# Keeping the turned input: one raw transpose of x, its norm factor applied afterwards, and the turned columns kept in DRAM for the residual

## The chip, the cores and the metric

The kernel runs on one core of one Trainium2 chip. The metric is the device time of one execution in microseconds. The time before is 1986.39 us, the median of three runs (1981.85, 1986.65 and 1986.39). "Faster", "same" and "slower" are told apart at 0.3% of that, about 6 us.

## What is computed

One layer of a hybrid decoder runs on two groups that share all weights: a prompt of 256 tokens and a sample group of 8 sequences with one token each, so 264 columns in all. In short:

```python
h = rmsnorm(x) * norm_mix                      # x: (256, 2048) prompt, (8, 2048) sample
q, k, v, z, xbc, dt, qm, gates = split(h @ w_in)
a_out = sliding_window_attention(q, k, v)      # 16 heads, 4 kv heads, window 128
s_out = ssd(xbc, z, dt)                        # Mamba-2 branch
m_out = cross_attention(qm, memory)            # memory = rmsnorm(mem_prompt) @ w_mem_kv
merged = g0 * (a_out @ w_up_swa) + g1 * (s_out @ w_up_ssd) + g2 * (m_out @ w_up_mem)
x = x + merged @ w_out                         # the residual: x itself is needed again here
x = x + (silu(rmsnorm(x) @ w_gate) * (rmsnorm(x) @ w_up)) @ w_down
```

All data are float32. The kernel keeps nearly float32 precision by splitting each operand of the large products into a rounded high part and a low part, and adding three products: high by high, high by low, low by high.

## The kernel before, in words

Activations are kept *turned*: the 2048 features lie on partitions, as `KT` = 16 blocks of 128, and the 264 tokens (256 prompt, `NP`; 8 sample, `NS`) lie along the free dimension. A large product is a list of *units*. One unit is 512 KB of weights (two blocks of 128 rows by 512 columns): a DMA on SP's queue into `raw` (four buffers), a copy on ScalarE that rounds it into `hi` (line 167, function `split`), a subtraction on VectorE that gives `lo` (line 168), and then 24 matmuls on TensorE (line 146), or 12 wider ones for the memory product. `feed(i)` runs ahead of unit `i`: it issues the loads of up to four units more and splits up to three.

The units stand in this order: 32 for the memory tokens' keys and values (`pmem`), then the products with `w_in` (`pin`) mixed with the three upward products (`pua`, `pum`, `pus`), then 32 for `w_out` (`pout`, four groups `i` of 512 output features), then the feed-forward part (`pg`, `pu`, `pdn`).

Everything that is not a large product is *side work*: generators in two lists, `side` and `slow`. After each unit the main loop gives `side` 1.0 and `slow` 0.75 of credit, and each `yield` of a generator takes some. That fixes the order in which instructions are written down; a scheduler then reorders them by their dependencies, their priority (the written order) and a model of the engines' times, and each engine runs its own resulting list in order. The first three tasks of `side` are `mem_norm`, `prep_x` and `consts`. `mem_norm` must be written before unit 7, `prep_x` before unit 30, `consts` before the first `pin` unit.

`prep_x` makes the split input of all `pin` products, `hh` and `hl` (16 blocks each of 128 by 264). Before the change it loads the rows of x into four tiles of 128 by 1024 and the sample's rows into two tiles of 8 by 1024, squares them on ScalarE with a row sum, gets the factor `r` = 1/sqrt(mean + eps) by a few small VectorE operations (`rsqrt`), multiplies the rows by it in place on VectorE, and then, for each block `k`, turns three pieces on TensorE (two of 128 by 128, one of 8 by 128) into one PSUM tile `xT`. From that ScalarE writes `hh(k)` (scaled by the norm gain) and VectorE writes `hl(k)`.

`load_x(i)`, which is called when group `i` of `w_out` begins, loads 512 columns of x once more, unscaled (`xg` and `xgs`), turns them by twelve transposes into PSUM tiles `xTr`, and copies them on ScalarE into `xT`, the residual that `after_out(i)` adds to the product.

Buffers that matter: `t1` (four tiles of 128 by 264), `t4` and `ev` (four tiles each of 128 by 4 by 264), and the PSUM tag `s` with three banks that all transposes and small matmuls share. `move_rows` copies two caches from DRAM to DRAM; it is written down with the last group of `w_out`.

Of the kernel before, what the change touches and what calls it, by code (L numbers as in the profile page):

```python
# [8 lines left out]
F32 = mybir.dt.float32  # L9
# [3 lines left out]
AF = mybir.ActivationFunctionType  # L13
ALU = mybir.AluOpType
AX = mybir.AxisListType
# [3 lines left out]
P = 128  # L19
D = 2048  # L20
NP = 256
NS = 8
NT = NP + NS
KT = D // P
# [48 lines left out]
def tile_hybrid_decoder_step(  # L73
# [9 lines left out]
    nc = tc.nc  # L83
    act = nc.scalar.activation
    V = nc.vector
# [6 lines left out]
    dr = ctx.enter_context(tc.tile_pool(name="dr", bufs=1, space=DRAM))  # L92
# [4 lines left out]
    def nm(s):  # L97
        uid[0] += 1
        return f"{s}_{uid[0]}"
# [4 lines left out]
    def t4(name, dt=F32):  # L104
        return tp.tile([P, 4 * NT], dt, tag="t4", name=nm(name), bufs=4)

    def ev(name):
        return tp.tile([P, 4, NT], F32, tag="ev", name=nm(name), bufs=4)
# [16 lines left out]
    def t2(name, dt=F32):  # L125
        n = 512 if dt in (F32, F32R) else 1024
        return tp.tile([P, n], dt, tag="t2", name=nm(name), bufs=4)

    def t1(name, dt=F32):
        return tp.tile([P, NT], dt, tag="t1", name=nm(name), bufs=4)  # L130

    def tiny(name, n):
        assert n <= 64
        return tp.tile([P, 64], F32, tag="tiny", name=nm(name), bufs=9)[:, 0:n]

    def const(shape, name, dt=F32, tag=None):
        return cp.tile(shape, dt, tag=tag or name, name=name)
# [4 lines left out]
    def sps(name):  # L142
        return pq.tile([P, 512], F32, tag="s", name=nm(name))

    def mm(out, lhsT, rhs, start=True, stop=True):
        nc.tensor.matmul(out, lhsT=lhsT, rhs=rhs, start=start, stop=stop)  # L146

    def tr(out, in_):
        n = in_.shape[0]
        nc.tensor.transpose(out, in_, ident[0:n, 0:n])  # L150

    def rsqrt(v, n, parts=P, alloc=None):

        alloc = alloc or tiny
        y = alloc("rs_y", n)[0:parts]
        a = alloc("rs_a", n)[0:parts]
        V.tensor_scalar(y.bitcast(I32), v.bitcast(I32), 1, None, op0=ALU.logical_shift_right)
        V.tensor_scalar(y.bitcast(I32), y.bitcast(I32), -1.0, MAGIC, op0=ALU.mult, op1=ALU.add)
        for _ in range(3):
            V.tensor_tensor(a, y, y, op=ALU.mult)  # L160
            V.scalar_tensor_tensor(a, a, -0.5, v, op0=ALU.mult, op1=ALU.mult)
            V.scalar_tensor_tensor(y, a, 1.5, y, op0=ALU.add, op1=ALU.mult)
        return y

    def split(hi, lo, src):

        act(hi, src, AF.Copy)  # L167
        V.tensor_tensor(lo, src, hi.bitcast(F32), op=ALU.subtract)  # L168


    ident = const([P, P], "ident")
    make_identity(nc, ident)
    ones = const([P, P], "ones")
# [19 lines left out]
    xs_rows = x_sample.rearrange("b s d -> (b s) d")  # L193
# [7 lines left out]
    g_mem, g_mix = vgc[:, 0:16], vgc[:, 16:32]  # L201
# [198 lines left out]

    hh, hl = Feat("hh"), Feat("hl")

    def prep_x():
        x_t = {}
        for h in range(2):
            for t in range(2):
                m = (lm if t else ld)("x")
                nc.gpsimd.dma_start(m, x_prompt[0, t * P:(t + 1) * P, h * 1024:(h + 1) * 1024])
                x_t[t, h] = m
                yield 1.3  # L410
        xs = {h: ev("xs").rearrange("p c n -> p (c n)")[0:NS, 0:1024] for h in range(2)}
        for h in range(2):
            nc.gpsimd.dma_start(xs[h], xs_rows[:, h * 1024:(h + 1) * 1024])
            x_t[2, h] = xs[h]
        jk = t2("jkx", BF16)
        ss = tiny("ssx", 6)
        V.memset(ss, 1.0)
        for t in range(3):
            n = P if t < 2 else NS
            for h in range(2):  # L420
                act(jk[0:n], x_t[t, h], AF.Square, accum_out=ss[0:n, 2 * t + h:2 * t + h + 1])
            yield 0.5
        v = tiny("vx", 3)
        V.tensor_tensor(v, ss[:, 0:6:2], ss[:, 1:6:2], op=ALU.add)
        V.tensor_scalar(v, v, 1.0 / D, EPS, op0=ALU.mult, op1=ALU.add)
        r = rsqrt(v, 3)
        yield 1.5
        for t in range(3):
            n = P if t < 2 else NS
            for h in range(2):  # L430
                V.tensor_scalar(x_t[t, h], x_t[t, h], r[0:n, t:t + 1], None, op0=ALU.mult)
            yield 1.2
        for k in range(KT):
            ps = sps("xT")
            h, c = k // 8, (k % 8) * P
            for t in range(3):
                n = P if t < 2 else NS
                tr(ps[:, t * P:t * P + n], x_t[t, h][:, c:c + P])
            act(hh(k), ps[:, 0:NT], AF.Copy, scale=g_mix[:, k:k + 1])
            V.scalar_tensor_tensor(hl(k), ps[:, 0:NT], g_mix[:, k:k + 1], hh(k).bitcast(F32),  # L440
                                   op0=ALU.mult, op1=ALU.subtract)
            yield 0.4


    tri = const([P, P], "tri")
# [989 lines left out]
    x2 = {}  # L1435

    def load_x(i):
        xt = t4("xg")[:, 0:1024].rearrange("p (t c) -> p t c", t=2)
        nc.gpsimd.dma_start(xt, x_prompt[0, :, 512 * i:512 * (i + 1)].rearrange("(t p) c -> p t c", p=P))
        xs = t2("xgs")[0:NS]  # L1440
        nc.gpsimd.dma_start(xs, xs_rows[:, 512 * i:512 * (i + 1)])
        o = t4("xT").rearrange("p (c n) -> p c n", c=4)
        for c in range(4):
            ps = sps("xTr")
            for t in range(2):
                tr(ps[:, t * P:(t + 1) * P], xt[:, t, c * P:(c + 1) * P])
            tr(ps[:, NP:NT], xs[:, c * P:(c + 1) * P])
            act(o[:, c], ps[:, 0:NT], AF.Copy)
        x2[f"r{i}"] = o

    def after_out(i):
# [28 lines left out]
    def before_out(i):  # L1480
        load_x(i)
        if i == 3:
            move_rows()
# [67 lines left out]

    side.add("m", mem_norm())
    side.add("x", prep_x())
    side.add("c", consts())
    side.add("Mp", mem_prompt_work(), ["qm"])
# [61 lines left out]
```

## Time and profile before

| | before |
|---|---|
| median of three runs | 1986.39 us |
| the profiled execution | 1981.87 us |
| its span, first to last instruction | 1980.1 us |
| TensorE matmuls busy | 1937.3 us, 98% of the span |
| VectorE busy | 1159.3 us, 59% |
| ScalarE busy | 970.8 us, 49% |
| GpSimd busy | 122.6 us, 6% |
| mean granted TensorE clock | 0.994 of full speed |
| moved by DMA | 400.78 MB, 202 GB/s |

In the lines of the profile PE is TensorE, PEld its weight loads, DVE VectorE, ACT ScalarE, POOL GpSimd and SP the engine whose queue issues the weight loads. "L146" is line 146 of the kernel. An arrow `out<-in` names the tile written and the tiles read. A window is given in microseconds from the first instruction.

### The profile page before, as it was taken

The page shows a single profiled execution, that of the slowest core. Times are in us where ns is not written, and L with a number is a line of the kernel's source. Part 1 is how long each engine was busy: PE and PEld are TensorE (multiplying, and loading weights), DVE is VectorE, ACT ScalarE, POOL GpSimd, SP SyncE. Part 2 cuts the span into 40 slices and gives each one's busy share as a digit, 9 for nine tenths or more (in the row PEclk, how much of TensorE's full clock was granted, in tenths as well). Part 3 has the DMA queues.
Part 4 walks back from the last instruction along what each step waited for, and adds up shares of the span by engine and source line. Part 5 has one row for each costly group of instructions (what it writes and reads, how often), then busy time and mean ns, then how long its engine had stood idle before and what let it go on. Part 6 is the DMA issues. An engine that isn't in the chain of part 4 may idle for free.

```text
span 1980.1 us, 37652 instructions
## 1 busy us (share of the span) xinstructions
PE 1937.3 (98%) x15436; PEld 1871.3 (95%) x15436; DVE 1159.3 (59%) x2217; ACT 970.8 (49%) x1419; POOL 122.6 (6%) x241
## 2 busy tenths in 40 slices
PE   8999999999898989999999999999999999999999
PEld 6799998889898989899999999999999999999998
DVE  6645577656486858568455556555545555445553
ACT  6544446656665575655444444444334444334443
POOL 3000110010101202111000000000000000000000
PEclk9999999999999999999999999999999999999999
DMA  8576677677678878779666556665556665566653
GB/s 283 192 221 206 204 210 232 199 220 232 172 203 223 249 195 252 243 268 334 186 192 191 183 164 178 181 181 180 181 181 174 184 185 180 182 179 180 181 188 130
DMA packets 190974, 400.78 MB, mean 202 GB/s; under 512 B 13491, under 2 KB 15714, under 8 KB 190664
## 3 DMA queue, kind: packets, MB, share of 16 engines
q1 hardware_dynamic: 169856, 324.13, 53.4%
q0 software_dynamic: 20944, 74.23, 12.6%
q8 instruction: 121, 1.98, 0.4%
q14 instruction: 53, 0.43, 0.1%
HBM read 376.53 MB, written 24.06 MB: 202 GB/s over the span
## 4 chain that ended last, share of the span: by engine, by line
PE 84%; DMA 7%; DVE 3%; issue 3%; ACT 1%; POOL 0%; SPq 0%; ACTq 0%; POOLq 0%
PE pin L146 22%; PE pu L146 13%; PE pdn L146 13%; PE pg L146 13%; PE pout L146 5%; PE pus L146 5%; PE pmem L146 5%; DMA raw<-in_w_in_dram 3%; PE pum L146 2%; DMA ld<-in_state_ssm_dram 1%; DVE lo L168 1%; PE pua L146 1%; DVE ld L1226 1%; DMA acs_d<-acsT 1%; PE po L146 1%
## 5 line engine op out<-in xcount | busy, mean ns | idle before, releaser
L168 DVE TENSOR_TENSOR lo<-raw,hi 128x1024 fp32r<-128x1024 f32 (+1 forms) x626 | 746.7, 1195 | 650.7 <-ACT hi L167 649.7
L167 ACT ACTIVATE hi<-raw 128x1024 fp32r<-128x1024 f32 (+1 forms) x626 | 646.0, 1036 | 869.4 <-PE pin L146 190.3
L146 PE MATMUL pin<-hh,hi 128*128 128x264 f32 x1728 | 494.7, 289 | 15.8 <-ACT hi L167 15.6
L146 PE MATMUL pin<-hl,hi 128*128 128x264 f32 x1728 | 493.3, 288 | 0.0
L146 PE MATMUL pin<-hh,lo 128*128 128x264 f32 x1728 | 483.7, 288 | 5.5 <-DVE lo L168 5.2
L146 PEld LDWEIGHTS pin<-hh,hi 128*128 128x128 f32 x1728 | 328.4, 190 | 22.9 <-ACT hi L167 18.2
L146 PEld LDWEIGHTS pin<-hh,lo 128*128 128x128 f32 x1728 | 322.2, 190 | 10.1 <-DVE lo L168 8.3
L146 PEld LDWEIGHTS pin<-hl,hi 128*128 128x128 f32 x1728 | 328.3, 190 | 3.3 <-issue 2.5
L146 PE MATMUL pdn<-fah,hi 128*128 128x264 f32 x704 | 199.7, 285 | 0.0
L146 PE MATMUL pdn<-fal,hi 128*128 128x264 f32 x704 | 199.4, 285 | 0.0
L146 PE MATMUL pu<-h2h,hi 128*128 128x264 f32 x704 | 199.4, 284 | 0.0
L146 PE MATMUL pu<-h2l,hi 128*128 128x264 f32 x704 | 199.3, 284 | 0.0
L146 PE MATMUL pg<-h2l,hi 128*128 128x264 f32 x704 | 199.1, 285 | 0.0
L146 PE MATMUL pg<-h2h,hi 128*128 128x264 f32 x704 | 198.4, 284 | 0.0
L146 PE MATMUL pdn<-fah,lo 128*128 128x264 f32 x704 | 197.0, 284 | 0.0
L146 PE MATMUL pu<-h2h,lo 128*128 128x264 f32 x704 | 196.6, 284 | 0.0
L146 PE MATMUL pg<-h2h,lo 128*128 128x264 f32 x704 | 196.1, 284 | 0.0
L146 PEld LDWEIGHTS pdn<-fah,hi 128*128 128x128 f32 x704 | 132.7, 189 | 0.1
L146 PEld LDWEIGHTS pu<-h2h,hi 128*128 128x128 f32 x704 | 132.7, 189 | 0.0
L146 PEld LDWEIGHTS pg<-h2h,hi 128*128 128x128 f32 x704 | 132.7, 188 | 0.0
L146 PEld LDWEIGHTS pdn<-fal,hi 128*128 128x128 f32 x704 | 132.6, 188 | 0.1
L146 PEld LDWEIGHTS pu<-h2l,hi 128*128 128x128 f32 x704 | 132.6, 188 | 0.0
(511 smaller groups left out, 2964.7 us busy)
## 6 DMA issues: line engine op xcount, KB each, us to landing
raw<-in_w_in_dram SPq DMA_DIRECT2D x218, 512.0 KB, 4.5
raw<-in_w_gate_dram SPq DMA_DIRECT2D x88, 512.0 KB, 3.7
raw<-in_w_up_dram SPq DMA_DIRECT2D x88, 512.0 KB, 3.9
raw<-in_w_down_dram SPq DMA_DIRECT2D x88, 512.0 KB, 4.0
raw<-in_w_mem_kv_dram SPq DMA_DIRECT2D x32, 512.0 KB, 5.2
raw<-in_w_up_ssd_dram SPq DMA_DIRECT2D x32, 512.0 KB, 3.8
raw<-in_w_out_dram SPq DMA_DIRECT2D x32, 512.0 KB, 3.7
ld<-in_cache_mem_k_dram POOLq DMA_DIRECT2D x16, 512.0 KB, 5.5
```

Source lines behind the costliest of these rows:

```text
L146: nc.tensor.matmul(out, lhsT=lhsT, rhs=rhs, start=start, stop=stop)
L167: act(hi, src, AF.Copy)
L168: V.tensor_tensor(lo, src, hi.bitcast(F32), op=ALU.subtract)
L1226: V.scalar_tensor_tensor(h[:, b], bb[:, b], dx[:, b:b + 1], h[:, b], op0=ALU.mult, op1=ALU.add)
```

## The change

`prep_x` turns x unscaled. The sample's 8 rows are loaded as one tile of 128 by 128 (16 pieces of 128 features for each of 8 rows, so partition 8k+b holds piece k of row b) and turned by one transpose into `xsT`. The sums of squares of the sample rows, which now lie spread over 16 partitions each, are gathered by a matmul of `ones` with a selection matrix `sel`; the prompt's factors are spread along the free dimension by a matmul of `ones` with a diagonal `dgx`. The result is one tile `rb` of 128 by 264 that holds the norm factor of each column. For each block two pieces are turned, ScalarE copies them to a tile `raw` (tag `xr`), VectorE multiplies by gain and `rb` into `xn`, and `split` makes `hh(k)` and `hl(k)`. Every four blocks the raw tile is written to a DRAM tensor `xT_d`. `load_x(i)` is now one load from `xT_d`.

```diff
+    xT_d = dr.tile([P, KT, NT], F32, name="xT_d")
     def prep_x():
         x_t = {}
+        xs = t1("xs")[:, 0:P]
+        nc.gpsimd.dma_start(xs, xs_rows.rearrange("b (k n) -> k b n", n=P))
         for h in range(2):
             for t in range(2):
                 ... (load of x_t[t, h], as before)
                 yield 1.3
-        xs = {h: ev("xs").rearrange("p c n -> p (c n)")[0:NS, 0:1024] for h in range(2)}
-        for h in range(2):
-            nc.gpsimd.dma_start(xs[h], xs_rows[:, h * 1024:(h + 1) * 1024])
-            x_t[2, h] = xs[h]
         jk = t2("jkx", BF16)
         ss = tiny("ssx", 6)
-        V.memset(ss, 1.0)
-        for t in range(3):
-            n = P if t < 2 else NS
+        act(jk[:, 0:P], xs, AF.Square, accum_out=ss[:, 4:5])
+        for t in range(2):
             for h in range(2):
-                act(jk[0:n], x_t[t, h], AF.Square, accum_out=ss[0:n, 2 * t + h:2 * t + h + 1])
+                act(jk, x_t[t, h], AF.Square, accum_out=ss[:, 2 * t + h:2 * t + h + 1])
             yield 0.5
+        sel = tiny("sel", NS)
+        V.tensor_reduce(sel, ident.rearrange("p (k b) -> p b k", b=NS), axis=AX.X, op=ALU.add)
+        V.tensor_scalar(sel, sel, ss[:, 4:5], None, op0=ALU.mult)
+        ps = sps("xn")
+        tr(ps[:, 0:P], xs)
+        mm(ps[:, P:P + NS], ones, sel)
+        v = tiny("vx", 10)
+        ... (prompt sums and the eight gathered sums into v)
+        xsT = t1("xsT")[:, 0:P]
+        act(xsT, ps[:, 0:P], AF.Copy)
         V.tensor_scalar(v, v, 1.0 / D, EPS, op0=ALU.mult, op1=ALU.add)
-        r = rsqrt(v, 3)
+        r = rsqrt(v, 10)
         yield 1.5
-        for t in range(3):
-            n = P if t < 2 else NS
-            for h in range(2):
-                V.tensor_scalar(x_t[t, h], x_t[t, h], r[0:n, t:t + 1], None, op0=ALU.mult)
-            yield 1.2
-        for k in range(KT):
-            ps = sps("xT")
-            h, c = k // 8, (k % 8) * P
-            for t in range(3):
-                n = P if t < 2 else NS
-                tr(ps[:, t * P:t * P + n], x_t[t, h][:, c:c + P])
-            act(hh(k), ps[:, 0:NT], AF.Copy, scale=g_mix[:, k:k + 1])
-            V.scalar_tensor_tensor(hl(k), ps[:, 0:NT], g_mix[:, k:k + 1], hh(k).bitcast(F32),
-                                   op0=ALU.mult, op1=ALU.subtract)
-            yield 0.4
+        dg = t1("dgx")[:, 0:256]
+        for t in range(2):
+            V.tensor_scalar(dg[:, t * P:(t + 1) * P], ident, r[:, t:t + 1], None, op0=ALU.mult)
+        ps = sps("rbx")
+        mm(ps[:, 0:NP], ones, dg)
+        rb = t1("rb")
+        act(rb[:, 0:NP], ps[:, 0:NP], AF.Copy)
+        V.tensor_copy(rb[:, NP:NT], r[:, 2:10])
+        yield 0.5
+        for q in range(4):
+            raw = ev("xr")
+            V.tensor_copy(raw[:, :, NP:NT], xsT[:, 32 * q:32 * q + 32].rearrange("p (c b) -> p c b", b=NS))
+            for c in range(4):
+                k = 4 * q + c
+                h, o = k // 8, (k % 8) * P
+                ps = sps("xT")
+                for t in range(2):
+                    tr(ps[:, t * P:(t + 1) * P], x_t[t, h][:, o:o + P])
+                act(raw[:, c, 0:NP], ps[:, 0:NP], AF.Copy)
+                tm = t1("xn")
+                V.scalar_tensor_tensor(tm, raw[:, c], g_mix[:, k:k + 1], rb, op0=ALU.mult, op1=ALU.mult)
+                split(hh(k), hl(k), tm)
+                yield 0.6
+            nc.gpsimd.dma_start(xT_d[:, 4 * q:4 * q + 4], raw)
...
     def load_x(i):
-        xt = t4("xg")[:, 0:1024].rearrange("p (t c) -> p t c", t=2)
-        nc.gpsimd.dma_start(xt, x_prompt[0, :, 512 * i:512 * (i + 1)].rearrange("(t p) c -> p t c", p=P))
-        xs = t2("xgs")[0:NS]
-        nc.gpsimd.dma_start(xs, xs_rows[:, 512 * i:512 * (i + 1)])
         o = t4("xT").rearrange("p (c n) -> p c n", c=4)
-        for c in range(4):
-            ps = sps("xTr")
-            for t in range(2):
-                tr(ps[:, t * P:(t + 1) * P], xt[:, t, c * P:(c + 1) * P])
-            tr(ps[:, NP:NT], xs[:, c * P:(c + 1) * P])
-            act(o[:, c], ps[:, 0:NT], AF.Copy)
+        nc.gpsimd.dma_start(o, xT_d[:, 4 * i:4 * i + 4])
         x2[f"r{i}"] = o
```

More of the change, by code (lines that the diff above doesn't have):

```diff
@@ L422, in prep_x @@
             yield 0.5
-        v = tiny("vx", 3)
-        V.tensor_tensor(v, ss[:, 0:6:2], ss[:, 1:6:2], op=ALU.add)
+        sel = tiny("sel", NS)
[5 more added lines that the diff above has]
+        v = tiny("vx", 10)
+        V.tensor_tensor(v[:, 0:2], ss[:, 0:4:2], ss[:, 1:4:2], op=ALU.add)
@@ L425, in prep_x @@
+        V.tensor_copy(v[:, 2:10], ps[:, P:P + NS])
+        xsT = t1("xsT")[:, 0:P]
+        act(xsT, ps[:, 0:P], AF.Copy)
         V.tensor_scalar(v, v, 1.0 / D, EPS, op0=ALU.mult, op1=ALU.add)
-        r = rsqrt(v, 3)
+        r = rsqrt(v, 10)
         yield 1.5
-        for t in range(3):
-            n = P if t < 2 else NS
-            for h in range(2):
-                V.tensor_scalar(x_t[t, h], x_t[t, h], r[0:n, t:t + 1], None, op0=ALU.mult)
-            yield 1.2
-        for k in range(KT):
-            ps = sps("xT")
-            h, c = k // 8, (k % 8) * P
-            for t in range(3):
-                n = P if t < 2 else NS
-                tr(ps[:, t * P:t * P + n], x_t[t, h][:, c:c + P])
-            act(hh(k), ps[:, 0:NT], AF.Copy, scale=g_mix[:, k:k + 1])
-            V.scalar_tensor_tensor(hl(k), ps[:, 0:NT], g_mix[:, k:k + 1], hh(k).bitcast(F32),
-                                   op0=ALU.mult, op1=ALU.subtract)
-            yield 0.4
+        dg = t1("dgx")[:, 0:256]
```

## The prediction

> **What bounds the kernel now.** I read the busy shares first, then the two stages that the change touches by windows, then what ends the waits there.
>
> ```profile
> PE 1937.3 (98%) x15436; PEld 1871.3 (95%) x15436; DVE 1159.3 (59%) x2217; ACT 970.8 (49%) x1419; POOL 122.6 (6%) x241
> 63.90:113.80 49.90, 49.90 (x228) 38.80 (x228) 31.37 (x56) 24.65 (x35) 3.89 (x7) 1.00 0.62 204
> 600.00:700.00 100.00, 89.09 (x750) 86.21 (x748) 69.90 (x208) 54.96 (x102) 16.92 (x20) 0.98 0.86 234
> 700.00:800.00 100.00, 93.02 (x777) 91.27 (x778) 67.89 (x176) 62.62 (x103) 12.80 (x16) 0.95 0.81 230
> 1094.00:1198.00 104.00, 104.00 (x828) 100.98 (x827) 57.01 (x82) 49.74 (x78) 1.42 (x2) 1.00 0.54 175
> ```
>
> The window columns are: length, then busy time of TensorE's matmuls, its weight loads, VectorE, ScalarE and GpSimd, the granted clock, the DMA share and GB/s. The first window is the stretch in which `prep_x` multiplies and turns x, the last is the `w_out` stage. In both TensorE has no idle time, VectorE and ScalarE are busy for half to two thirds, DMA for 0.62 and 0.54. TensorE has gaps between 600 and 800, where the change writes nothing. A busy matmul row is modelled, so I ask who waits for whom (engine, line, releaser: total, times, longest):
>
> ```profile
> ACT hi L167 <- PE pmem L146: 20.4, 14, 1.9
> ACT hi L167 <- PE pout L146: 43.2, 23, 1.9
> ```
>
> These are the waits of 60 to 130 us and of the `w_out` stage. The rounding of the next weights waits until matmuls have released a `hi` buffer; so TensorE sets the pace, and not the load or the split. Time taken off TensorE's list in these two stages is time off the kernel, and nothing else in them is, as long as TensorE has its operands.
>
> **The change: TensorE.** The chain of waits runs through TensorE there, so its pieces (start, duration) are what the transposes cost on the path, without the overlap that single rows carry. First the shares by line of 76 to 122 us and of 1050 to 1230 us, then pieces:
>
> ```profile
> by line: PE pmem L146 69.0%; PE xT L150 14.3%; PE pin L146 11.8%; PE scT L150 3.5%; PE kmT L150 1.9%
> by line: PE pout L146 53.2%; PE pus L146 25.3%; PE pg L146 13.0%; PE pu L146 4.5%; PE xTr L150 4.0%; PE ss L146 0.2%
> 80.52 0.87 PE kmT L150 x8
> 81.39 0.37 PE xT L150 x3
> 114.14 0.89 PE xT L150 x6
> 116.44 0.38 PE xT L150 x3
> 174.03 0.22 PE ssT L150 x2
> 174.25 0.22 PE ssT L146 x4
> 213.36 1.30 PE scm L146 x6
> 1095.38 1.42 PE xTr L150 x9
> 1100.17 0.37 PE xTr L150 x3
> 1172.52 1.42 PE xTr L150 x9
> 1177.80 0.37 PE xTr L150 x3
> ```
>
> - *`w_out` stage, removed:* four groups, each 1.42 + 0.37 = 1.79 us for twelve transposes, together 7.16 us (the share says the same: 4.0% of 180 us is 7.2). A load takes their place, so all 7.16 us go.
> - *`prep_x`, removed:* 14.3% of 46 us is 6.6 us for 48 transposes; the pieces (eight of 0.37 or 0.38, four of 0.89) add to 6.5. What stays is two 128 by 128 transposes for each of 16 blocks. Two such cost 0.22 (`ssT` x2), and eight cost 0.87, which is the same for each. 16 x 0.22 = 3.5. Saved: 3.0 us.
> - *`prep_x`, added:* one transpose of `xs`, 0.87 / 8 = 0.11; `ones` by `dgx`, 256 columns as in `scm`, 1.30 / 6 = 0.22; `ones` by `sel`, 8 columns, between a `ssT` product of one column (0.055) and the 0.22 of 256 columns; I take 0.1, since 8 is nearer to 1. Together 0.43 us.
>
> Sum on TensorE: 7.16 + 3.0 - 0.43 = 9.7 us, from 9.6 to 9.8 by the one bounded price.
>
> **ScalarE and VectorE in `prep_x`.** They cost nothing only while they hide under TensorE. The rows (count: min/median/max ns, first and last start):
>
> ```profile
> L439 ACT ACTIVATE hh<-xT,vgc x16: 462/482/499, 82.9 to 116.9; 128x264 fp32r<-128x264 f32 x16
> L440 DVE SCALAR_TENSOR_TENSOR hl<-xT,vgc,hh x16: 481/486/494, 83.5 to 117.4; 128x264 fp32r<-128x264 f32 x16
> L1448 ACT ACTIVATE xT<-xTr x16: 368/380/393, 1096.6 to 1178.2; 128x264 f32<-128x264 f32 x16
> L167 ACT ACTIVATE mg<-mgs x16: 405/410/432, 1025.7 to 1098.0; 128x264 fp32r<-128x264 f32 x16
> L168 DVE TENSOR_TENSOR mg<-mgs,mg x16: 420/423/426, 1027.6 to 1099.2; 128x264 fp32r<-128x264 f32 x16
> L431 DVE TENSOR_SCALAR x<-x,rs_y x4: 764/767/767, 64.2 to 66.2; 128x1024 f32<-128x1024 f32 x4
> L421 ACT ACTIVATE jkx<-xs x2: 1041/1042/1042, 54.9 to 56.9; 8x1024 bf16<-8x1024 f32 x2
> ```
>
> Per block ScalarE gives up `hh` from PSUM (0.48) and takes a raw copy (like L1448, 0.38) and a rounding (like `mg`, 0.41): +0.31, 16 blocks +5.0 us; the two squares of 8 rows go (2 x 1.04), against one of 128 columns and two small copies of about 0.3 each. Net some +4 us. VectorE gives up `hl` (0.49) and takes the multiply by gain and `rb` (the same kind, 0.49) and a subtraction (0.42): +6.8 us; the in-place multiplies go (4 x 0.77, and two of 8 rows at about the same), and some 1.5 us of small operations come (`sel`, `dgx`, the sample columns). Net about +4 us. Idle in the first window were 49.9 - 31.4 = 18.5 us on VectorE and 25.2 on ScalarE. So both hide. In the `w_out` stage ScalarE loses 16 x 0.38 = 6.1 us, off the path: nothing.
>
> The raw transposes need no norm factor, so they can start before it is known, and by the credits the first block is written 3.6 units earlier: 8.2 of credit stand ahead of it instead of 11.8.
>
> **DMA.** Added are four writes of 128 x 4224 B = 541 KB on GpSimd's queue, 2.16 MB in all, while the first blocks of weights for `pin` arrive; the reloads in the `w_out` stage stay as large (528 KB each, from `xT_d` instead of x). The sample's rows come in 512 B pieces, 64 KB as before. What hides the writes is the lead of the weight loads:
>
> ```profile
> 95.96 1.06 ACT L167 ACTIVATE hi<-raw 128x1024 fp32r<-128x1024 f32 x1 [0.88 <-PE pmem L146]
> ...
> 110.46 1.06 ACT L167 ACTIVATE hi<-raw 128x1024 fp32r<-128x1024 f32 x1 [1.81 <-PE pmem L146]
> 97.05 1.23 DVE L168 TENSOR_TENSOR lo<-raw,hi 128x1024 fp32r<-128x1024 f32 x1 [1.44 <-ACT hi L167]
> 98.30 3.73 SPq L230 DMA_DIRECT2D raw<-in_w_in_dram  x2
> DMA to landing us min/median/max: 3.5/4.6/5.9
> ```
>
> The buffer rounded at 95.96 and subtracted until 98.3 is loaded anew at 98.30 and needed four units later, at 110.46: 12.2 us, and a load lands in 3.5 to 5.9 (60 to 130 us). A weight load that had to wait for a whole write as long as itself would land after at most 11.8. So I put the writes at 0. Behind a write on GpSimd's queue stand the cache loads that wait for the same x tiles anyway, and output stores.
>
> The Trainium skill, page "DMA: Bandwidth & Descriptors", section "Queues, rings and completion order", says that each DMA engine takes turns between the queues that have work, a packet at a time. By that rule a weight load beside a write gets half of the engines and lands about twice as late, near 9 us by the median row; that is still inside the 12.2, so the sum would come out the same, and the rule speaks against the change only if loads already stood at the edge. No row of before has a store of this size in this stretch.
>
> **The residual's load.** The tile now needs one `t4` buffer instead of two:
>
> ```profile
> 1026.87 0.71 POOL L1439 DMA_DIRECT2D xg<-in_x_prompt_dram  x1 [97.57 <-DVE mgs L1426]
> 1126.89 0.72 POOL L1439 DMA_DIRECT2D xg<-in_x_prompt_dram  x1 [25.49 <-PE xTr L150]
> ```
>
> The first load was issued when the first `mgi` tile was released, the last when the transposes of an earlier group had released theirs. Without these transposes each of the four loads follows an `mgi`, the last at about 1098, and the first is needed only by the addition at the end of the group, 20 us or more after. Cost 0. What is late next after the transposes: nothing in these 104 us; `hi` again waits for TensorE.
>
> **The sum.** 1981.87 us (profiled execution, span 1980.1) - 9.7 = 1972.2. The profiled execution is the lowest of the three runs within 0.02 us; their median, 1986.39, is 4.5 higher and another run stands beside it. Which of the two levels the median falls on cannot be read from one trace; the gain is the same from either, and I forecast from the median: 1986.39 - 9.7 = 1976.7, a change of -0.49%.
>
> **The rivals.**
>
> - *Part of the `prep_x` gain is lost in a TensorE wait.* TensorE runs its list in order, and two new small products wait for ScalarE's and VectorE's statistics. If the scheduler's model of these is too short, all matmuls behind wait. The rows for such waits:
>
> ```profile
> PE pmT L150 <- DVE pm L642: 2.2, 2, 1.2
> PE xtok L150 <- ACT xs L979: 5.0, 1, 5.0
> ```
>
>   Two waits of 1.2 us give -7.3 us (1979.1), two of 5.0 give +0.3 (no change). Against it: between 63.9 and 113.8 the same kind of chain (`rsqrt`, `km`, `kmT`) left no idle time.
> - *The writes do delay the weights.* If each of the four makes one weight load land 2 us beyond its 12.2, 8 us come back: 1984.7. It decides only from a landing of 12 us, twice the longest row.
> - *Slower: the blocks of `hh` and `hl` come too late for the first `pin` units.* The factor tile `rb` and `xsT` hold two of four `t1` buffers through the loop, so `xn` has two at most; with one (a constants' tile takes the other), a block takes multiply, rounding, subtraction in series (0.49 + 0.41 + 0.42) and waits behind one weight rounding and one subtraction (1.06 + 1.23): 3.6 us. Sixteen take 58 us. `pin` needs its last two blocks seven units after its start, 113.8 + 7 x 2.9 = 134 us. From a first block at 81, as before, the last comes at 139 and costs 5 us; from 92 on, 16 us, more than the gain and 6 us beside: 1986.39 + 6 = 1992.7. Against it: the first block should start earlier than 81, and VectorE's and ScalarE's idle time allow about 1.7 blocks in each unit, 16 in 27 us.
> - *The middle falls out another way.* Every instruction list is laid out anew, and the stretch from 600 to 800 hangs on when bursts of state loads meet weight loads:
>
> ```profile
> 613.41 20.63 DMA raw<-in_w_in_dram
> 681.42 18.36 DMA raw<-in_w_in_dram
> 784.43 20.03 DMA raw<-in_w_in_dram
> ```
>
>   TensorE idles 10.9 + 7.0 = 17.9 us there, 6.0 for each of these three landings. One or two more: 1982.7 or 1988.7, no change that can be told; one fewer: 1970.7.
>
> **How the numbers follow.** Forecast as worked out, within 5 us: 0.62. Part lost in a TensorE wait: 0.10. Writes delay weights: 0.06. Blocks too late: 0.09. More late landings in the middle: 0.08, fewer: 0.05. Faster by over 0.3%, about 6 us and what a measurement of this kernel can tell: 0.58 of the forecast's 0.62, 0.05 of the TensorE wait's, and the fewer landings, 0.68. Slower: the late blocks and a rest, 0.10. Same: 0.22. The likeliest case's own range is 1969 to 1980, from the lower run level less the sum and 3 us to the upper one and 3. For 8 in 10 it reaches up over the lost part and the delayed weights to 1985, and down to 1968; left out are the late blocks, most of the worse middle and a little below.
>
> **What would show it.** Right: no `xTr` rows at all; `xT` with 32 transposes in TensorE's part of the chain, about 3.5 us; groups of `pout` about 23.9 us apart where they were 25.7; TensorE without idle time from 64 to 140 us; weight landings under 12 us there. Wrong: idle time of TensorE before `xn`, `rbx` or the first `pin` products; rounding waits on weight loads near the `xT_d` stores; or stages between 140 and 1090 us that take longer than before although the change does nothing in them.

## The result: 1972.46 us, 0.6% faster

| | before | after |
|---|---|---|
| median | 1984.6 us (five runs) | 1972.46 us (five runs, 1969.11 to 1975.83) |
| profiled execution | 1981.87 us | 1972.57 us |
| its span | 1980.1 us | 1970.8 us |
| ratio to before, 95% interval | | 0.9941 (0.9929 to 0.9954) |

The forecast was 1976.7 us and a gain of 9.7; the medians differ by 12.1 us, and the interval of the ratio stands for 9 to 14 us. A second measurement of the same kernel (below) gave 0.9922 (0.9907 to 0.9936).

The page of the kernel after, its busy shares, and then the windows of the two changed stages (length, busy TensorE matmuls, weight loads, VectorE, ScalarE, GpSimd, granted clock, DMA share, GB/s):

```profile
PE 1924.3 (98%) x15377; PEld 1865.2 (95%) x15377; DVE 1163.9 (59%) x2236; ACT 967.5 (49%) x1419; POOL 121.5 (6%) x240
64.00:140.00 76.00, 76.00 (x474) 67.20 (x473) 48.36 (x89) 44.65 (x79) 9.16 (x17) 1.00 0.77 246
1094.00:1189.00 95.00, 95.00 (x778) 95.00 (x777) 57.00 (x82) 45.06 (x63) 1.61 (x3) 1.00 0.64 207
```

TensorE still has no idle time in either stage, while VectorE and ScalarE have room; the added work on them is hidden. Over the whole kernel the matmuls' busy time fell by 13.0 us, the span by 9.3.

To see where the time went I use a clock that both kernels share: the starts of VectorE's 626 weight subtractions (`lo<-raw,hi`, line 168), numbered from 0. The same number stands at the same place of the large products in every kernel here. The table gives the length of each stretch, in us.

| subtraction | what runs | before | after | difference |
|---|---|---|---|---|
| 0 to 24 | memory product, first units | 68.62 | 68.63 | 0.0 |
| 24 to 40 | end of `prep_x`, first `pin` units | 56.87 | 51.42 | -5.45 |
| 40 to 56 | `pin` alone | 37.29 | 37.30 | 0.0 |
| 56 to 328 | attention, state space, upward products | 911.58 | 915.45 | +3.9 |
| 328 to 368 | `w_out` | 126.70 | 117.90 | -8.80 |
| 368 to 624 | feed-forward | 752.01 | 752.02 | 0.0 |

The first subtraction starts at 10.25 us before and at 11.38 after. So the two stages gave 14.25 us, not 9.7, and a stretch in which nothing was to change took 3.9 back in this pair of profiles.

The chain of waits follows the last instruction back, at each step to what released it. After the change, in the same stages (start, duration, what):

```profile
82.53 0.22 PE xT L150 x2
82.75 5.33 PE pmem L146 x23
88.08 0.22 PE xT L150 x2
88.30 0.23 PE pmem L146
88.54 0.44 PE xT L150 x4
...
1079.99 14.95 PE pus L146 x122
1094.94 94.05 PE pout L146 x768
1188.99 7.75 PE pg L146 x64
```

There are no `xTr` pieces, 768 products of `w_out` stand in one run, and a group takes 94.05 / 4 = 23.5 us where I had expected 23.9. A pair of transposes costs the 0.22 us that I had priced. What I had not priced shows beside them. Three rows of the chain before, in the same place:

```profile
87.07 0.37 PE xT L150 x3
87.44 0.43 PE pmem L146
87.87 0.37 PE xT L150 x3
```

One `pmem` matmul between two runs of transposes takes 0.43 us before and 0.23 after. The run of three, which ends with the 8-row transpose, costs its own 0.37 and another 0.2 in the matmul behind it. With 12 such runs in `prep_x` and 8 in `w_out` that is 2.4 and 1.6 us more than my sum, 5.4 and 8.8 us in all. The experiments test this as theory A.

### The profile page after: what moved, and what is told of

Its sections match the earlier page's. It is cut to its first block, busy times and chain, and to the rows that moved or that the text cites. A ratio compares the mean times of both kernels' runs of the same rounds, so it can differ in the third digit from the quotient of the medians.

```text
span 1970.8 us, 37564 instructions
## 1 busy us (share of the span) xinstructions
PE 1924.3 (98%) x15377; PEld 1865.2 (95%) x15377; DVE 1163.9 (59%) x2236; ACT 967.5 (49%) x1419; POOL 121.5 (6%) x240
## 4 chain that ended last, share of the span: by engine, by line
PE 84%; DMA 8%; issue 3%; DVE 3%; ACT 1%; POOL 0%; SPq 0%; ACTq 0%; POOLq 0%
PE pin L146 23%; PE pu L146 13%; PE pdn L146 13%; PE pg L146 13%; PE pus L146 5%; PE pout L146 5%; PE pmem L146 5%; DMA raw<-in_w_in_dram 3%; PE pum L146 2%; DMA ld<-in_state_ssm_dram 1%; PE pua L146 1%; DVE lo L168 1%; DMA ld<-in_cache_mem_k_dram 1%; DMA acs_d<-acsT 1%; PE po L146 1%
```

## The experiments

**Each half by itself.** `load_x` of before is replaced by one load (residual from other data), with everything else of before:

```diff
-        (loads xg, xgs, twelve transposes into xTr, four copies)
+        nc.gpsimd.dma_start(o, x_prompt[0, 63 * i:63 * i + 66].rearrange("s d -> (s d)").rearrange("(p c n) -> p c n", p=P, c=4))
```

> The kernel before with only the w_out part of the change: load_x is one load of the same size and shape, from rows of x_prompt as they lie in memory (so the residual that is added is not x; the store of xT_d and the new prep_x are left out). Theory A (a transpose of 8 rows costs TensorE about 0.15 us itself and another 0.2 us in the matmul that follows a run of transposes): the w_out stage is 8.8 us shorter than before, the groups of pout 23.5 us apart instead of 25.7, the whole about 1984.6 - 8.8 = 1975.8. Rival B (the chain's pieces of 1.42 + 0.37 us per group are the whole price, as predicted, and what the change gained beyond 9.7 us is scatter of the middle of the kernel): the stage is 7.2 us shorter, 23.9 us a group, the whole about 1977.4. Rival C (part of the gain of w_out hangs on the new prep_x): less than 5 us.

Measured: stretch 328 to 368 117.90 us, -8.80, as in the kernel after; 24 to 40 unchanged at 56.87. Median 1973.89, ratio 0.9943 (0.9927 to 0.9959), so 8 to 14 us faster. Theory A has the stage right at 8.8 us; B is 1.6 us off, and C falls, as the `w_out` part needs nothing of the other.

The other half, the kernel after with the old `load_x`:

```diff
-        nc.gpsimd.dma_start(o, xT_d[:, 4 * i:4 * i + 4])
+        (load_x of before)
```

> The kernel after with the load_x of before, so only the prep_x part of the change; the four stores to xT_d are still made, and nothing reads them. Theory A: the stretch up to the 40th weight subtraction is 4 to 5.5 us shorter than before, the whole about 1984.6 - 5 = 1979.6, and the w_out groups are 25.7 us apart as before. Rival B: 2.6 us shorter, about 1982. If the late first matmul of the changed kernel (1.1 us later than before) belongs to the change, it is seen here too; if it is scatter of the first loads, it may be gone.

Measured: 24 to 40 51.42 us, -5.45 again; `w_out` 126.70, as before. Median 1981.85, ratio 0.9986 (0.9976 to 0.9996): a gain of 1 to 5 us, less than I expected from A, since 56 to 328 took 917.09 us here, 5.5 more than in the profile of before. The first subtraction started late here too, at 11.88 us, but also in the run before this one, at 11.49 with the old `prep_x`; so the late start does not come with the new one.

**The shape of the sample's transposes.** The kernel before with sample tiles of full height:

```diff
-        xs = t2("xgs")[0:NS]
-        nc.gpsimd.dma_start(xs, xs_rows[:, 512 * i:512 * (i + 1)])
+        xs = t2("xgs")
+        nc.gpsimd.memset(xs, 0.0)
+        nc.gpsimd.dma_start(xs[0:NS], xs_rows[:, 512 * i:512 * (i + 1)])
...
-            tr(ps[:, NP:NT], xs[:, c * P:(c + 1) * P])
+            tr(ps[:, NP:NP + P], xs[:, c * P:(c + 1) * P])
 (the same in prep_x)
```

> The kernel before, but each sample tile is filled with zeros below its 8 rows and turned as 128 by 128, in prep_x and in load_x; nothing else is changed, and the number of transposes stays at 48 and 48. Theory A (the 8-row transposes are dear because of their shape): 48 x 0.109 = 5.2 us in each of the two stages instead of 8.9 and 8.8, so about 7.3 us faster than before, 1977.3, with the w_out groups 24.8 us apart. Rival B (the price is that of any transpose, 0.37 us for three): 48 x (0.123 - 0.109), 1.3 us faster in all, 1983.3, groups 25.4 to 25.7 us apart. Rival E (any switch between weight matmuls and transposes costs the 0.2 us, whatever the shape): also about 1.3 us.

Measured: 53.18 us from 24 to 40 (-3.69, A said 8.9 - 5.2 = 3.7), 123.19 in `w_out` (-3.51, A said 3.6), median 1977.69, ratio 0.9963 (0.995 to 0.9976). B and E, 1.3 us in all, are out. Turning sixteen times as many rows, most of them zeros, made the kernel before some 7 us faster. Its chain, with the same number of transposes:

```profile
86.74 0.33 PE xT L150 x3
87.06 0.23 PE pmem L146
87.30 0.33 PE xT L150 x3
```

The matmul between two runs is back at 0.23.

**The price of one transpose.** Into the kernel after, 160 extra transposes, one after each of 160 feed-forward units, where the stretch 368 to 624 otherwise repeats to 0.03 us:

```diff
         u["prod"](hi, lo)
+        if len(units) - 256 <= i < len(units) - 96:
+            tr(sps("dose")[:, 0:8], hi[0:8, 0:P].bitcast(F32))      # dose_8
+            tr(sps("dose")[:, 0:64], hi[0:64, 0:P].bitcast(F32))    # dose_64
+            tr(sps("dose")[:, 0:P], hi[:, 0:P].bitcast(F32))        # dose_128
+            tr(sps("dose")[0:8, 0:P], hi[:, 0:8].bitcast(F32))      # dose_cols
```

(one of the four lines in each kernel, one execution of each)

> The kernel after with 160 extra transposes in the feed-forward stage, one after each of 160 units, each of 8 rows by 128 columns of the unit's own hi tile into an unused PSUM tile. TensorE is never idle there, so the stage grows by 160 times the price of one such transpose between weight matmuls. Theory A: 0.35 us each, 56 us in all. Rival B: 0.15 us each, 24 us. Rival E (the switch costs 0.2 us whatever the shape): 0.35 us here too, but 0.31 with 128 rows.

> As the run with 8 rows, but each extra transpose is 128 rows by 128 columns. Theory A: 0.109 us each, 17.4 us in all. Rival B: 0.109 us each too. Rival E: about 0.31 us each, 50 us.

> As the run with 8 rows, but each extra transpose is 64 rows by 128 columns. If what is dear is any transpose that does not fill the rows: 0.3 us or more each, about 50 us. If it is the small number of rows alone: near 0.11 us each, 18 us.

> As the run with 8 rows, but each extra transpose is 128 rows by 8 columns. If what is dear is unfilled rows only: 0.11 us or less each, at most 18 us. If any transpose smaller than the array is dear: about 0.35 us each, 56 us.

| transposed piece | stretch 368 to 624 longer by | each |
|---|---|---|
| 8 rows x 128 | 55.8 us | 0.349 us |
| 64 rows x 128 | 64.7 us | 0.405 us |
| 128 rows x 128 | 17.85 us | 0.112 us |
| 128 rows x 8 | 17.9 us | 0.112 us |

The chain of waits of three of them, in the order 8, 64 and 128 rows:

```profile
1301.96 0.15 PE dose L150
1302.11 3.12 PE pg L146 x24
1305.24 0.15 PE dose L150
```

```profile
1302.78 0.21 PE dose L150
1302.98 3.11 PE pg L146 x24
1306.09 0.20 PE dose L150
```

```profile
1301.87 0.11 PE dose L150
1301.98 2.92 PE pg L146 x24
1304.90 0.11 PE dose L150
```

The piece itself costs 0.15, 0.20 or 0.11 us. The 24 matmuls of the unit behind it take 3.12 us after 8 or 64 rows and 2.92 after 128: the missing 0.20, booked on other work. B and E are out, and so is "the few rows": 64 are dearer than 8. In the shapes tried, what is dear is a transpose that leaves rows of the array unused, between work that uses all; one that leaves columns unused pays nothing.

With 8 or 64 rows the second operand, the identity, is also only 8 or 64 columns wide (`8*128 8x8` and `64*128 64x64` in their rows), so the extra transposes alone do not tell few rows from a narrow second operand. The kernel after has a product that does: `ssys` has all 128 rows and a second operand of 32 columns (two rows in the trace):

```profile
944.20 0.28 PE L146 MATMUL pin<-hh,lo 128*128 128x264 f32 x1
944.33 0.30 PE L146 MATMUL ssys<-ys,ones 128*128 128x32 f32 x2
944.47 0.37 PE L146 MATMUL pin<-hh,hi 128*128 128x264 f32 x1
944.67 0.28 PE L146 MATMUL pin<-hl,hi 128*128 128x264 f32 x1
```

The `pin` matmuls before it start 0.12 us apart. From the first row to the last are 0.47 us, where two such distances take 0.25. That leaves 0.22 us for the two `ssys` rows, 0.11 each, and nothing like 0.20 on top. So a narrow second operand is not what is dear; the unused rows are.

The Trainium skill, page "TensorEngine Tiling (Array Packing)", section "Key Properties", says that changing the tiling mode drains TensorE. The runs fit that for rows, with 0.20 us behind each such transpose; that the mode is what changes there, no row of a trace says. With 128 rows by 8 columns they show no such cost, whether because such a piece changes no mode or because that change is free; no run here tells these apart.

**The stores.** The kernel after without them (load as in the first experiment):

```diff
-            nc.gpsimd.dma_start(xT_d[:, 4 * q:4 * q + 4], raw)
```

> The kernel after without the four stores to xT_d; load_x loads the same amount from rows of x_prompt as they lie in memory, so the residual that is added is not x. Theory A and the prediction: the stores are hidden by the lead of the weight loads, the time is that of the kernel after, 1972.5, within 2 us, and the longest weight landing from 60 to 130 us falls from 9.5 to about 6 us with no gain from it. Rival D (the stores delay the weights or the cache loads behind them on GpSimd's queue): 2 us or more faster than after.

Measured: median 1969.64, ratio 0.9921 (0.9906 to 0.9935), 2.8 us below the first median of the kernel after, as rival D has it and A does not. So I ran it again beside the kernel after and one that makes each store twice:

```diff
+    xT_e = dr.tile([P, KT, NT], F32, name="xT_e")
...
+            nc.gpsimd.dma_start(xT_e[:, 4 * q:4 * q + 4], raw)
```

> The kernel after, unchanged, once more beside the two runs about its stores. The stages up to the 24th, from the 24th to the 40th and from the 328th to the 368th weight subtraction: as in the first profile to 0.05 us for the last two (5.45 and 8.81 us shorter than before). From the 56th to the 328th: scatter of some us, 1.5 to 5 us longer than in the profile of before, if that profile was a lucky one of its kernel. Ratio to before 0.993 to 0.995.

> The kernel after without the four stores to xT_d, unchanged (the residual that is added is not x). TensorE's order is the same as in the kernel after, only the four stores are missing from GpSimd's queue. Theory A (the stores are hidden; the 2.8 us by which the first run was faster are scatter of the middle): the time is that of after_again within 1.5 us. Rival D (the stores cost some 3 us): again 2.5 us or more faster than after_again.

> The kernel after with each of the four stores made twice, the second to a DRAM tensor that nothing reads: 2.16 MB more on GpSimd's queue in the same stretch. Theory A (stores hidden by the 12.2 us lead of the weight loads): the time of after_again within 1.5 us, though the longest weight landing from 60 to 130 us grows beyond 9.5 us; a stall only if it passes 12.2. Rival D (the stores cost some 3 us): some 3 us slower than after_again.

| | median | ratio to before (95%) | 24 to 40 | 56 to 328 |
|---|---|---|---|---|
| after, again | 1969.87 us | 0.9922 (0.9907 to 0.9936) | 51.42 | 911.93 |
| no store, again | 1969.45 us | 0.9913 (0.9899 to 0.9927) | 51.42 | 910.77 |
| store twice | 1966.03 us | 0.9898 (0.9881 to 0.9915) | 52.10 | 908.69 |

No cost of the stores is left in the medians: without them 0.4 us faster, as A said; with twice as many 3.8 us faster, where D wanted 3 us slower and A the same time within 1.5. For the kernel after itself two expectations missed: the ratio was 0.9922, below 0.993, and 56 to 328 was 0.4 us longer than in the profile of before, not 1.5 to 5.

The landing times of weight loads from 60 to 130 us (min, median, max), of no store (first run), after (first profile) and store twice:

```profile
DMA to landing us min/median/max: 3.5/4.3/8.3
```

```profile
DMA to landing us min/median/max: 3.6/4.7/9.5
```

```profile
DMA to landing us min/median/max: 3.4/4.7/12.9
```

Then the waits of the roundings for weights, of the second profile of after (60 to 130 us, longest landing 11.3) and of store twice (100 to 140 us), and store twice's window of 64 to 140 us:

```profile
ACT hi L167 <- DMA raw<-in_w_in_dram: 4.9, 3, 2.5
```

```profile
ACT hi L167 <- DMA raw<-in_w_in_dram: 12.1, 7, 2.7
64.00:140.00 76.00, 76.00 (x475) 67.25 (x474) 48.08 (x89) 44.79 (x79) 12.36 (x21) 1.00 0.79 275
```

At 9.5 no rounding waited for a weight load. At 11.3 three did, though the lead was to be 12.2 us; yet 24 to 40 was again 51.42. The 12.2 came from one buffer. In the same profile of before a load issued at 125.3 us is rounded at 134.6, 9.3 us later, and in the kernel after the loads issued from 94 to 130 us are rounded 9.3 to 11.9 us after their issue.

With the stores doubled, seven roundings waited, and subtraction 38 came 3.4 us later than in the kernel after. Subtraction 40 came 0.68 us later, which is all that the 52.10 says: subtraction 41 was on time again, 54.34 us after subtraction 24 in both, and TensorE had no idle time. So not even the doubled stores cost anything here. I take what hid them to be a second margin, that `feed` rounds up to three units ahead of the matmuls; no run used that margin up.

**The kernel before, against itself.**

> The kernel before, unchanged, against itself. Theory A: its stage from the 24th to the 40th and from the 328th to the 368th weight subtraction repeats to 0.05 us, and the stretch from the 56th to the 328th differs from the first profile's by some us, since that profile (1981.87 us) is among the fastest of its kernel and the median of the other runs lies near 1986. Rival F (the middle of the kernel before is steady, so the longer middle in profiles of the kernel after belongs to the change): within 1 us of the first profile there. Ratio 1 within its interval.

Measured: ratio 1.0001 (0.9989 to 1.0013); 24 to 40 56.86, `w_out` 126.70, 56 to 328 912.03. The profile of 56 to 328 repeats to 0.5 us, as rival F had it; the scatter of some us that theory A expected did not show in these two profiles. The stretch 0 to 24 took 69.92 us, 1.3 more than in the first profile, so that much is scatter of the first loads.

## Why the prediction was right

The forecast of 1976.7 us lies 4.2 us above the first measurement, and its gain of 9.7 inside the interval of 9 to 14. That the number came so close is partly luck: the two stages gave 14.25 us where the sum has 7.16 + 3.0 for them, and in the first pair of profiles the middle of the kernel took 3.9 back. The kind of gain and its two places were right; two terms were mis-sized.

*What bounds.* Right: TensorE's list is the path in both stages, and what left it left their time. The stretch of `w_out` is 117.90 us in all ten runs without its transposes, and 24 to 40 is 51.42 in all with the new `prep_x` except store twice, whose difference is made up one subtraction later.

*`w_out`, 7.16 us.* Right in kind, too small: 8.80. The term that was mis-sized is the price of a run of transposes. I summed the runs' own pieces and left out what they cost the matmul behind: 8 runs at 0.2.

*`prep_x`, 3.0 us saved.* Too small for the same reason: 5.45, from 12 runs at 0.2. The rows with the single matmul of 0.43 us between two runs stood in the view that I summed, and I did not read them.

*Added products, 0.43 us.* Wrong in a price that did not matter: `ones` by `dgx` alone takes 0.43, since a float32 product has two rows in the trace and I had divided the 1.30 us of `scm` x6 by six instead of three.

```profile
L146 PE MATMUL rbx<-dgx,ones x2: 377/380/382, 67.6 to 67.8; 128*128 128x256 f32 x2
```

It falls into the stretch 0 to 24, whose scatter of 1.3 us is larger. TensorE did not wait for it: the rival with a wait there did not come.

*ScalarE, VectorE, the late blocks.* Right: TensorE did not wait for them, and over the whole kernel VectorE was busy 4.6 us longer and ScalarE 3.3 us less, near the +4 and 4 - 6.1 of the prediction. The first block did not come earlier, as I had said, but at 82.5 us behind the transposes `kmT`; the last was turned at 109.3, and `pin` began 2.7 us earlier than before. The rival of the late blocks has a slip in its sum, 1986.39 + 6 is 1992.4 and not 1992.7.

*DMA.* Right in the outcome, the stores cost nothing; wrong in the margin. The lead of 12.2 us was read from one buffer and is 9.3 to 11.9 in the kernel after, so a landing of 11.3 already made roundings wait. TensorE had its operands all the same. The rival in which a landing beyond 12.2 costs 2 us each was tried by the doubled stores: the longest landing was 12.9, and it cost nothing. The Trainium skill, page "DMA: Bandwidth & Descriptors", section "Queues, rings and completion order", has the engines take turns between queues; the estimate of near 9 us stands beside longest landings of 9.5 and 11.3 measured. But 8.3 was reached without the stores, and the median stayed at 4.3 to 4.7, so these runs do not test the rule.

*The residual's load.* Right: the four loads follow the release of `mgi` (its releaser is the subtraction `mgs` in these rows), the last at 1097.

```profile
1026.44 0.56 POOL L1457 DMA_DIRECT2D xT<-xT_d  x1 [92.86 <-DVE mgs L1444]
...
1097.02 0.53 POOL L1457 DMA_DIRECT2D xT<-xT_d  x1 [23.00 <-DVE mgs L1444]
1097.54 0.56 POOL L541 DMA_DIRECT2D out_dram<-in_cache_swa_k_dram  x1
```

The last row is a move that I did not foresee: the copies of `move_rows` were issued at 882 us before, and stand behind the residual's loads now. In the stretch 264 to 288, which lies there, the four profiles with the copies at about 882 (before twice, prep alone, padded rows) took 72.3 to 73.1 us; the ten with the copies at 1090 to 1101 took 69.0 to 71.3, with one of 74.2. That fits a relief of some 2.4 us, but TensorE's and VectorE's order changed there too, and no run moved the copies alone.

*The middle.* The rival of an unlucky middle partly came in the profiles, and with it one of the prediction's own signs of being wrong, a longer stage between 140 and 1090 us. The six profiled executions with the instruction lists of the kernel after (two of after, four with extra transposes behind) took 911.9 to 916.2 us from 56 to 328, on average 2.7 more than the two of before. The medians do not show it: they differ by 12.1 and 16.6 us, around the 14.25 of the two stages. Part of it lies from 56 to 264. There seven of the eight profiles with stores took 724.7 us or more, and all six without 723.8 or less. But the eighth, with twice the stores, took 721.90, and the medians of after_again and no_store_again are 0.4 us apart. So more stores do not make this stretch longer; what makes it vary, and what pays it back in the medians, stays open.

No run points to a version that is surely better than the changed kernel. Store twice has a median 3.8 us below after_again, and its profile is 3.2 us shorter from 56 to 328, where the second store changes nothing that I can name; the two intervals overlap.

## What to carry to other kernels

Where TensorE's list is the path, price an operation by the distance between two equal pieces of the surrounding work, once with it and once without; its own row, and its own piece of the chain, leave out what it costs its neighbour. Look for short operations that use only some of the array's rows and stand alone between full ones: gather them (as here, 128 sample pieces in one transpose) or fill the rows with zeros. For an added transfer, compare the landing times with the lead of the loads beside it, load by load and not from one row. Then ask how far the work behind those loads runs ahead: here the roundings waited up to 2.7 us each for late weights, and the engine that bounds did not wait at all.

## What the runs showed of the hardware that was not expected

A transpose of 8 or 64 rows between full matmuls costs 0.35 or 0.40 us in all, 0.20 of it in the matmuls behind; one of 128 rows by 128, or by 8 columns, costs 0.112 us and nothing behind. A float32 product of 128 rows with a second operand of only 32 columns has no such cost either (0.22 us for its two rows in the trace). A float32 product of 256 columns takes 0.43 us of TensorE and stands in the trace as two rows.
